# A state space scan laid out by channels, two heads side by side in the array's columns

## The chip, the cores and the metric

The kernel runs on one core of a Trainium2 chip. The metric is the device time of one execution in microseconds (us). The engines are TensorE (PE in the profile; its weight loads are PEld), VectorE (DVE), ScalarE (ACT), GpSimd (POOL) and SyncE (SP, which here only issues transfers). Each runs its own queue in order.

## The reference

One decoder layer for 256 tokens (T) of width 2048. The part that changes is the state space branch: 32 heads of 64 channels in 8 groups of 4 heads, each group with its own B and C of 128 states. All 256 tokens are one chunk, so the scan is one masked product:

```python
a_dt = dt * a                                  # a = -exp(a_log), per head
a_cum = cumsum(a_dt)                           # along the tokens
decay_in = exp(where(l >= s, a_cum[l] - a_cum[s], -inf))
cb = einsum('lgn,sgn->gls', c_in, b_in)
y = einsum('gls,gels,sgep->lgep', cb, decay_in, x * dt)
y = y + d_skip * x
g = y * silu(z)                                # 2048 channels in 8 groups of 256
o_ssd = g * rsqrt(mean(g * g, group) + 1e-6) * ssd_norm_w
...
merged = g_sb * (o_sb @ w_branch_sb) + g_ssd * (o_ssd @ w_branch_ssd) + g_mem * (o_mem @ w_branch_mem)
```

Before it come an RMSNorm and one wide input projection (for z, x, B, C, the other branches and the gates); beside it stand two attention branches, behind it an output projection, a residual and a last RMSNorm.

## The kernel before, in words

**Weights and gemms.** All weights stream from memory as fp32, 512 KB a chunk. A chunk is split into two fp32r parts: ScalarE copies `raw` to `wh`, VectorE subtracts and writes `wl` (`split`). Four `raw` buffers and three of each part are in use in turn. Two helpers multiply:

- `gemm` (rows: tokens on the output's partitions) holds 128 tokens of the activations still and streams 512 weight columns, three matmuls for each k tile and half of the tokens (L264 to L266). A chunk has two k tiles, 12 matmuls.
- `gemm_cols` (columns: channels on the output's partitions) holds 128 x 128 weights still and streams the tokens: two matmuls of 512 columns (both parts of the activations) and two of 256 (L227, L231) for each k tile. A chunk has four k tiles. The two accumulators are added by `fold`, one ScalarE copy and one VectorE addition for 256 channels.

**Order.** The order of all engines' work is the order in which the Python code issues it. After each chunk a gemm calls `pump()`: it runs what `defer` put off for so many chunks (the evacuations, the SiLUs), and then one step of one of two `lanes`. A lane is a queue of generators, and each `yield` ends a step, so small work is strewn between the chunks. Even chunks serve one lane, odd chunks the other. `finish()` runs what is left in the lanes without chunks between.

**The state space branch.** z is projected by `gemm` (rows, 4 calls) into `zD`, and x, B and C by `gemm_cols` (columns) with a causal convolution of four taps into `cT`; SiLU follows on both. `start_ssd` then puts 8 `ssd_group` generators and 8 `ssd_cols` into the lanes; they run between the chunks of the gates and branch products of the memory and stick-breaking branches. A group transposes x to rows (`xp`), loads the cumulated log decays of its four heads spread over all partitions (`dec`, from a small tensor `acT` in memory), makes the decays of the two diagonal 128 x 128 blocks (add, minimum, Exp), weighs them with the masked product of B and C (`cb`, `cbm`), and multiplies with x times dt (`xs`) into `y`, a matmul of 64 columns per head and block. The block below the diagonal needs no array of decays: x times dt is scaled by `edge[:, 0]`, multiplied once for all four heads (`off`), and scaled by `edge[:, 1]`. Then come the skip (`drow`), the gate, the sum of squares per token and 1 / rms by a power on GpSimd (`rsqrt_mean`). `ssd_cols` transposes the result back to columns (`dot`) and splits it into `oD`, the activations of `w_branch_ssd`.

Names with `wh`, `wl`, `acc` in the rows are the gemms; `hT`, `oM`, `oS`, `oD` and `mT` are their activations; `sig` are the gates, `merged` the sum of the branches.

Of the kernel before, what the change touches and what calls it, by code (L numbers as in the profile page):

```python
# [41 lines left out]
def trunk_kernel(  # L42
# [3 lines left out]
    d_skip, w_mem_kv, w_branch_sb, w_branch_ssd, w_branch_mem,  # L46
# [46 lines left out]
    wcols = const.tile([P, 192], F32, name="wcols")  # L93
    normw, ssdw, convb = wcols[:, 0:16], wcols[:, 16:32], wcols[:, 32:64]
    convw = wcols[:, 64:192].rearrange("p (j i) -> p j i", i=32)

# [27 lines left out]
    drow = const.tile([P, SSD_HEADS], F32, name="drow")  # L124

# [6 lines left out]
    edge = const.tile([P, 2, SSD_HEADS], F32, name="edge")  # L132
# [222 lines left out]
    def along(k):  # L355
# [14 lines left out]
        if k == 6:  # L370
            nc.sync.dma_start(wcols, w_cols)
            nc.sync.dma_start(drow, d_skip.partition_broadcast(P))
# [74 lines left out]
    def dt_steps():  # L447
# [222 lines left out]
    zD = [slot([P, D], F32, "zD") for _ in range(2)]  # L670

    def z_evac(c0):
        def evac(acc):
            for t in range(2):
                nc.scalar.activation(zD[t][:, c0:c0 + GW], acc[t], AF.Copy)
        return evac

    for g in range(4):
        gemm(hT, NKT, w_in, C_SSDZ + g * GW, z_evac(g * GW))
# [20 lines left out]
    waiting = [zD[i // 2][:, (i % 2) * 1024:(i % 2 + 1) * 1024] for i in range(4)]  # L700
# [11 lines left out]

    def ssd_group(g):
        heads = slice(4 * g, 4 * g + 4)
        cs = slice(g * T, (g + 1) * T)
        xp = bank([P, 2, T], "xp")
        for b in range(2):
            i = 2 * g + b
            for t in range(2):
                nc.tensor.transpose(xp[:, t, b * P:(b + 1) * P],  # L720
                                    cT[i // 8][:, i % 8, t * P:(t + 1) * P], ident)
        dec = []
        for h0 in (4 * g, 4 * g + 2):
            d = ta([P, 2, 2, P], "dec")
            nc.scalar.dma_start(d.rearrange("p h q t -> p h (q t)"),
                                acT[h0:h0 + 2].partition_broadcast(P))
            dec.append(d)
        yield
        xn = tb([P, 2, T], "xn")
        nc.scalar.activation(xn, xp, AF.Copy)  # L730
        xs = tb([P, 2, T], "xs")
        xe = tq([P, 3, P], "xe")
        by_head = lambda a: a.rearrange("p (h c) -> p h c", c=64)
        wide = lambda a: a[:, heads].unsqueeze(2).to_broadcast([P, 4, 64])
        xoff = xe[:, 0:2].rearrange("p a b -> p (a b)")
        for t in range(2):
            nc.gpsimd.tensor_tensor(by_head(xs[:, t]), by_head(xn[:, t]), wide(dts[:, t]),
                                    ALU.mult)
            nc.gpsimd.tensor_tensor(by_head(xn[:, t]), by_head(xn[:, t]), wide(drow), ALU.mult)
        nc.gpsimd.tensor_tensor(by_head(xoff), by_head(xs[:, 0]), wide(edge[:, 0]), ALU.mult)  # L740
        cb = bank([P, 4, P], "cb")
        bT, cTT = cT[2], cT[3]
        nc.tensor.matmul(cb[:, 0:2], bT[:, g, 0:P], cTT[:, g], start=True, stop=True)
        nc.tensor.matmul(cb[:, 2], bT[:, g, P:T], cTT[:, g, P:T], start=True, stop=True)
        yield

        for i, d in enumerate(dec):
            for e in range(2):
                for q in range(2):
                    h = 4 * g + 2 * i + e  # L750
                    nc.vector.tensor_scalar(d[:, e, q], d[:, e, q], nac[:, q, h:h + 1], 0.0,
                                            ALU.add, ALU.min)
        yield
        for d in dec:
            nc.scalar.activation(d, d, AF.Exp)
        yield
        nc.scalar.activation(xe[:, 2], cb[:, 1], AF.Copy)
        cbm = small2([P, 2, P], "cbm")
        nc.vector.tensor_tensor(cbm, cb[:, 0:3:2], past.unsqueeze(1).to_broadcast([P, 2, P]),
                                ALU.mult)  # L760
        for d in dec:
            nc.vector.tensor_tensor(d, d, cbm.unsqueeze(1).to_broadcast([P, 2, 2, P]),
                                    ALU.mult)
        yield
        y = bank([P, 2, T], "y")
        for e in range(4):
            xc = slice(e * 64, (e + 1) * 64)
            for q in range(2):
                nc.tensor.matmul(y[:, q, xc], dec[e // 2][:, e % 2, q], xs[:, q, xc], start=True, stop=True)  # L769
        off = bank([P, T], "off")  # L770
        nc.tensor.matmul(off, xe[:, 2], xoff, start=True, stop=True)  # L771
        yield
        nc.vector.tensor_tensor(by_head(xoff), by_head(off), wide(edge[:, 1]), ALU.mult)
        nc.vector.tensor_tensor(xn[:, 1], xn[:, 1], xoff, ALU.add)
        nc.vector.tensor_tensor(xn, y, xn, ALU.add)
        ss = small([P, 2], "gss")
        for t in range(2):
            nc.vector.tensor_tensor(xn[:, t], xn[:, t], zD[t][:, cs], ALU.mult)
        yield
        for t in range(2):  # L780
            nc.scalar.activation(xs[:, t], xn[:, t], AF.Square, accum_out=ss[:, t:t + 1])
        rs = small([P, 2], "grs")
        rsqrt_mean(rs, ss, T, 2)
        yield
        for t in range(2):
            nc.scalar.activation(zD[t][:, cs], xn[:, t], AF.Copy, scale=rs[:, t:t + 1])
        ssd_done.append(g)
        yield

    def ssd_cols(g):  # L790
# [4 lines left out]
        ot = bank([P, 2, T], "dot")  # L795
        for b in range(2):
            c = (2 * g + b) * P
            for t in range(2):
                nc.tensor.transpose(ot[:, b, t * P:(t + 1) * P], zD[t][:, c:c + P], ident)  # L799
        yield  # L800
        split(*[(*oD[0].at(2 * g + b), ot[:, b], ssdw[:, 2 * g + b:2 * g + b + 1])
                for b in range(2)])
# [22 lines left out]
    def gate_evac(c0, sig):  # L825
        nc.scalar.dma_start(sig[:, 0], b_gate[c0:c0 + GW].partition_broadcast(P))
        def evac(acc):
            for t in (1, 0):
                nc.vector.tensor_tensor(sig[:, t], acc[t], sig[:, 0], ALU.add)
            defer(lambda: nc.scalar.activation(sig, sig, AF.Sigmoid), 1)  # L830
# [18 lines left out]
    for br, (g0, src, nk, wb) in enumerate(branches):  # L849
        if br == 2:  # L850
            finish()
            mT.append(Cols(NKT, "mT"))
            src = oD[0]
        for g in range(4):
            sig = t4([P, 2, GW], "sig")
            gemm(hT, NKT, w_in, C_GATE + g0 + g * GW, gate_evac(g0 + g * GW, sig))
            gemm(src, nk, wb, g * GW, branch_evac(br, g, sig))
# [86 lines left out]
_INS = ['x', 'mem', 'x_cols', 'mem_cols', 'w_cols', 'w_in', 'b_gate', 'dt_bias', 'a_log', 'd_skip',  # L944
# [5 lines left out]
def lay_out(inputs):  # L950
# [10 lines left out]
    a['mem_cols'] = _np.concatenate([a['mem_norm_w'].reshape(-1, P).T, a['mem_cols']], axis=1)  # L961
    a['w_cols'] = _np.concatenate([a[n].reshape(-1, P).T for n in
# [19 lines left out]
```

## Time and profile before

| what | value |
|---|---|
| median of 3 runs | 1231.93 us (1231.27 to 1232.45) |
| profiled execution | 1232.29 us, span 1230.6 us |
| granted TensorE clock | 0.998 |
| busy: TensorE, its weight loads | 99%, 84% of the span |
| busy: VectorE, ScalarE, GpSimd | 62%, 50%, 7% |
| transfers | 240.58 MB, 196 GB/s |
| z projection (`zD`) | about 395 to 482 us |
| the groups and `ssd_cols` on TensorE | 685 to 948 us |

Busy time is a union over overlapping instructions. Matmuls are pipelined, and their recorded ends are modelled: two that follow each other overlap in the records, so the cost of one in a full queue is the distance from its start to the next start. An fp32 matmul is recorded as two passes, each with a weight load of its own. A row of the time order has the start, the duration, the engine, the line, the output and inputs, the tile sizes and the number of merged instructions; a row of waits has who waited, for whom, and the total, number and longest.

### The profile page before, as it was taken

Reading aid. Unit: us, or ns where it says so; the run is one execution under the profiler, and the core shown is the slowest. Engines: PE = TensorE matmul, PEld = TensorE weight load, DVE = VectorE, ACT = ScalarE, POOL = GpSimd, SP = SyncE. Lnnn points to the kernel's source line nnn. Section 1 sums busy time; section 2 is a strip of 40 time slices with the busy share of each in tenths; the row PEclk is TensorE's granted clock in tenths of the full one; section 3 lists DMA queues with packets and bytes.
Section 4 is the critical chain, followed back from the end, with each engine's and each line's share of the span. In section 5 each row is a group of like instructions: output and inputs, shape, how many; then the busy total and the mean of one; then the engine's idle time right before and its main releaser. Section 6 shows DMA issues by size and latency. Waiting matters only on the chain.

```text
span 1230.6 us, 16254 instructions
## 1 busy us (share of the span) xinstructions
PE 1220.5 (99%) x6228; PEld 1037.9 (84%) x6228; DVE 769.0 (62%) x999; ACT 617.2 (50%) x797; POOL 92.2 (7%) x104
## 2 busy tenths in 40 slices
PE   9999999999999999999999999999999999999997
PEld 7888888888888888888888888888888888888886
DVE  5686554565654555888878767576756554555554
ACT  6765544554444554545664655455555444444443
POOL 0000000000000000010000202123101110110101
PEclk9999999999999999999999999999999999999999
DMA  9966566655566665655666756666565666567673
GB/s 339 334 198 188 163 195 189 187 168 166 165 183 191 178 177 179 184 176 171 178 182 201 226 178 207 204 191 198 180 186 180 198 197 200 187 197 243 205 243 109
DMA packets 165789, 240.58 MB, mean 196 GB/s; under 512 B 10288, under 2 KB 93392, under 8 KB 165584
## 3 DMA queue, kind: packets, MB, share of 16 engines
q1 hardware_dynamic: 157152, 223.88, 58.9%
q10 hardware_dynamic: 8560, 15.67, 3.8%
q8 instruction: 48, 0.79, 0.3%
q14 instruction: 29, 0.24, 0.1%
HBM read 237.40 MB, written 2.13 MB: 195 GB/s over the span
## 4 chain that ended last, share of the span: by engine, by line
PE 95%; DMA 2%; issue 1%; ACT 1%; DVE 1%; SPq 0%; POOLq 0%; POOL 0%; ACTq 0%
PE acc L227 24%; PE acc L264 17%; PE acc L266 17%; PE acc L265 17%; PE acc L231 12%; PE y L769 1%; PE acc L400 1%; PE acc L401 1%; PE acc L399 1%; DMA raw<-in_w_out_dram 1%; DMA rows<-in_mem_dram 1%; DMA raw<-in_w_mem_kv_dram 0%; PE off L771 0%; PE dtp L459 0%; PE dot L799 0%
## 5 line engine op out<-in xcount | busy, mean ns | idle before, releaser
L148 DVE TENSOR_TENSOR wl<-raw,wh 128x1024 fp32r<-128x1024 f32 (+1 forms) x409 | 506.0, 1240 | 326.4 <-ACT wh L144 324.1
L144 ACT ACTIVATE wh<-raw 128x1024 fp32r<-128x1024 f32 (+1 forms) x409 | 431.5, 1056 | 423.7 <-PE acc L266 253.7
L227 PE MATMUL acc<-hT,wh 128*128 128x512 f32 x1152 | 363.2, 397 | 0.0
L231 PEld LDWEIGHTS acc<-hT,wl 128*128 128x128 f32 x1152 | 216.4, 188 | 51.2
L264 PE MATMUL acc<-wh,hT 128*128 128x512 f32 x576 | 227.8, 395 | 0.0
L231 PE MATMUL acc<-hT,wl 128*128 128x256 f32 x1152 | 226.5, 278 | 0.0
L266 PE MATMUL acc<-wh,hT 128*128 128x512 f32 x576 | 224.5, 390 | 0.0
L265 PE MATMUL acc<-wl,hT 128*128 128x512 f32 x576 | 224.4, 390 | 0.0
L227 PEld LDWEIGHTS acc<-hT,wh 128*128 128x128 f32 x1152 | 175.5, 189 | 0.1
L266 PEld LDWEIGHTS acc<-wh,hT 128*128 128x128 f32 x576 | 108.1, 188 | 22.9
L265 PEld LDWEIGHTS acc<-wl,hT 128*128 128x128 f32 x576 | 108.3, 188 | 21.8
L264 PEld LDWEIGHTS acc<-wh,hT 128*128 128x128 f32 x576 | 108.2, 188 | 21.7
L265 PE MATMUL acc<-wl,oD 128*128 128x512 f32 x128 | 49.8, 389 | 0.0
L266 PE MATMUL acc<-wh,oD 128*128 128x512 f32 x128 | 49.8, 389 | 0.0
L264 PE MATMUL acc<-wh,oD 128*128 128x512 f32 x128 | 49.8, 389 | 0.0
L695 DVE SCALAR_TENSOR_TENSOR cT<-cu,wcols,cT 128x255 f32<-128x255 f32 (+2 forms) x96 | 46.4, 483 | 3.4
L841 POOL TENSOR_TENSOR merged<-merged,sig 128x512 f32<-128x512 f32 x16 | 27.5, 1743 | 260.7 <-DVE sig L840 233.9
L631 POOL TENSOR_TENSOR lm<-lm,sp 128x384 f32<-128x384 f32 x8 | 11.5, 1432 | 394.5 <-DVE sp L630 392.4
L227 PE MATMUL acc<-memT,wh 128*128 128x512 f32 x128 | 40.6, 398 | 0.0
L264 PE MATMUL acc<-wh,mT 128*128 128x512 f32 x96 | 37.4, 390 | 0.0
L266 PE MATMUL acc<-wh,mT 128*128 128x512 f32 x96 | 37.4, 389 | 0.0
L265 PE MATMUL acc<-wl,mT 128*128 128x512 f32 x96 | 37.4, 389 | 0.0
(250 smaller groups left out, 1306.1 us busy)
## 6 DMA issues: line engine op xcount, KB each, us to landing
raw<-in_w_in_dram SPq DMA_DIRECT2D x288, 512.0 KB, 3.8
raw<-in_w_branch_ssd_dram SPq DMA_DIRECT2D x32, 512.0 KB, 4.0
raw<-in_w_out_dram SPq DMA_DIRECT2D x32, 512.0 KB, 4.9
raw<-in_w_mem_kv_dram SPq DMA_DIRECT2D x31, 512.0 KB, 6.3
raw<-in_w_branch_mem_dram SPq DMA_DIRECT2D x16, 512.0 KB, 4.8
raw<-in_w_branch_sb_dram SPq DMA_DIRECT2D x16, 512.0 KB, 4.3
dec<-acT ACTq DMA_DIRECT2D x16, 256.0 KB, 5.6
sig<-in_b_gate_dram ACTq DMA_DIRECT2D x12, 256.0 KB, 3.9
```

What stands on the lines that cost most here:

```text
L144: nc.scalar.activation(hi, src, AF.Copy, **({} if scale is None else {"scale": scale}))
L148: nc.vector.tensor_tensor(lo, src, h32, ALU.subtract)
L227: nc.tensor.matmul(halves[b], wh[:, kt - k0, b * P:(b + 1) * P], lhs.both(kt), start=first, stop=False, skip_group_check=True)
L231: nc.tensor.matmul(halves[b][:, 1], wl[:, kt - k0, b * P:(b + 1) * P], lhs.at(kt)[0], start=False, stop=last, skip_group_check=True)
L264: nc.tensor.matmul(a, lh[:, tt], wh[:, j], start=first, stop=False)
L265: nc.tensor.matmul(a, lh[:, tt], wl[:, j], start=False, stop=False)
L266: nc.tensor.matmul(a, ll[:, tt], wh[:, j], start=False, stop=last)
L399: nc.tensor.matmul(a, lh[:, tt], wh[:, g], start=first, stop=False)
L400: nc.tensor.matmul(a, lh[:, tt], wl[:, g], start=False, stop=False)
L401: nc.tensor.matmul(a, ll[:, tt], wh[:, g], start=False, stop=last)
L695: nc.vector.scalar_tensor_tensor(a[:, s:T], u[:, 0:T - s], convw[:, 3 - s, i:i + 1], a[:, s:T], ALU.mult, ALU.add)
L841: nc.gpsimd.tensor_tensor(merged[t][:, cs], merged[t][:, cs], sig[:, t], ALU.add)
```

## The change

The state space branch now stays in columns. z is projected by `gemm_cols` into `zT`. In a group, x is still transposed for use as the stationary operand, but now x times dt (64 columns of a head) is held still and the weighed decays are streamed, so `y` comes out with channels on partitions: two heads go to partitions 0 to 63 and 64 to 127 of the output, that is to the two halves of the array's columns. The decays of the block below the diagonal are made like the others (`nacx` in place of `edge`), three blocks a head; the four heads' blocks lie in three tiles `dec`, one of them from another pool. The loads of `dec` are issued by SP instead of ScalarE, five of 128 or 64 KB instead of two of 256 KB. The skip is one VectorE operation per 128 channels with a column `dcol` that comes with `wcols`. The sum of squares over the 256 channels of a group is now one across partitions: squares, an addition, a split, and two matmuls with ones (`rb`) into `tot`. 1 / rms is exp(-0.5 ln(ms)) on ScalarE and one step of Newton's on VectorE, both on 128 x 256 elements. `ssd_cols` has no transposes any more. `exp_ln` loads the table that has both Exp and Ln if a Sigmoid has been there since. `finish()` and the allocation of `mT` stand behind the first gate product of the third branch instead of ahead of it.

```diff
-    zD = [slot([P, D], F32, "zD") for _ in range(2)]
...
-    for g in range(4):
-        gemm(hT, NKT, w_in, C_SSDZ + g * GW, z_evac(g * GW))
+    zT = [slot([P, 8, T], F32, "zT") for _ in range(2)]
+    for g in range(8):
+        gemm_cols(hT, NKT, w_in, C_SSDZ + 2 * g * P, to_cols(zT[g // 4], 2 * (g % 4)))
...
-        nc.vector.tensor_tensor(edge[:, 0], nac[:, 0], ps[:, 2], ALU.subtract)
-        nc.vector.tensor_scalar(edge[:, 1], nac[:, 1], -1.0, None, ALU.mult)
-        nc.scalar.activation(edge, edge, AF.Exp)
+        nc.vector.tensor_tensor(nacx, nac[:, 0], ps[:, 2], ALU.subtract)
...
+    def exp_ln():
+        if not tables[0]:
+            nc.scalar.preload_act_table_set("natural_log_exp_and_others")
+            tables[0] = True
...
     def ssd_group(g):
+        dec = [ta([P, 4, P], "dec"), ta([P, 4, P], "dec"), tb([P, 4, P], "dec")]
+        block = lambda e, j: dec[e][:, j] if e < 3 else dec[j][:, 3]
+        for e in range(3):
+            nc.sync.dma_start(dec[e][:, 0:2].rearrange("p q t -> p (q t)"),
+                              acT[heads[e]:heads[e] + 1].partition_broadcast(P))
+        for j in range(2):
+            nc.sync.dma_start(dec[j][:, 3:4], acT[heads[3]:heads[3] + 1,
+                                                  j * P:(j + 1) * P].partition_broadcast(P))
...
+        nc.vector.tensor_tensor(by_head(xs), by_head(xp), dts[:, :, heads[0]:heads[0] + 4]
+                                .unsqueeze(3).to_broadcast([P, 2, 4, 64]), ALU.mult)
...
+        def log_decays(e):
+            for j, i, a in ((2, 1, nac[:, 1]), (1, 1, nacx), (0, 0, nac[:, 0])):
+                nc.vector.tensor_scalar(block(e, j), block(e, i), a[:, heads[e]:heads[e] + 1],
+                                        0.0, ALU.add, ALU.min)
+        def weigh(i):
+            nc.vector.tensor_tensor(dec[i][:, 0:3], dec[i][:, 0:3], cbm, ALU.mult)
+            nc.vector.tensor_tensor(dec[i][:, 3], dec[i][:, 3], cbm[:, i], ALU.mult)
...
         y = bank([P, 2, T], "y")
-        for e in range(4):
-            xc = slice(e * 64, (e + 1) * 64)
-            for q in range(2):
-                nc.tensor.matmul(y[:, q, xc], dec[e // 2][:, e % 2, q], xs[:, q, xc], start=True, stop=True)
-        off = bank([P, T], "off")
-        nc.tensor.matmul(off, xe[:, 2], xoff, start=True, stop=True)
+        for b in range(2):
+            pair = [(e, y[64 * (e % 2):64 * (e % 2) + 64, b]) for e in (2 * b, 2 * b + 1)]
+            xe = lambda e, t: xs[:, t, 64 * e:64 * e + 64]
+            for e, o in pair:
+                if e < 3:
+                    nc.tensor.matmul(o, xe(e, 0), dec[e][:, 0:2], start=True, stop=False,
+                                     skip_group_check=True)
+                else:
+                    for j in range(2):
+                        nc.tensor.matmul(o[:, j * P:(j + 1) * P], xe(e, 0), block(e, j),
+                                         start=(j == 0), stop=False, skip_group_check=True)
+            for e, o in pair:
+                nc.tensor.matmul(o[:, P:T], xe(e, 1), block(e, 2), start=False, stop=True,
+                                 skip_group_check=True)
...
+            nc.vector.scalar_tensor_tensor(xT[b], xT[b], dcol[:, i:i + 1], y[:, b], ALU.mult,
+                                           ALU.add)
...
+        nc.vector.tensor_tensor(zg, zg, xg, ALU.mult)
+        nc.scalar.activation(xs, zg, AF.Square)
+        yield
+        nc.vector.tensor_tensor(xs[:, 0], xs[:, 0], xs[:, 1], ALU.add)
+        sq = tmp.tile([P, 2, T], F32R, tag="tq", name=nm("sq"), bufs=2)
+        split((sq[:, 0], sq[:, 1], xs[:, 0], None))
+        yield
+        tot = bank([P, T], "tot")
+        for i in range(2):
+            nc.tensor.matmul(tot, rb, sq[:, i], start=(i == 0), stop=(i == 1))
+        yield
+        ms, rs = xs[:, 0], xs[:, 1]
+        nc.vector.tensor_scalar(ms, tot, 1.0 / T, EPS, ALU.mult, ALU.add)
+        exp_ln()
+        nc.scalar.activation(rs, ms, AF.Ln)
+        nc.scalar.activation(rs, rs, AF.Exp, scale=-0.5)
+        yield
+        nc.vector.tensor_tensor(ms, ms, rs, ALU.mult)
+        nc.vector.tensor_tensor(ms, ms, rs, ALU.mult)
+        nc.vector.tensor_scalar(ms, ms, -0.5, 1.5, ALU.mult, ALU.add)
+        nc.vector.tensor_tensor(rs, rs, ms, ALU.mult)
+        nc.vector.tensor_tensor(zg, zg, xs[:, 1:2].to_broadcast([P, 2, T]), ALU.mult)
...
     def ssd_cols(g):
-            for t in range(2):
-                nc.tensor.transpose(ot[:, b, t * P:(t + 1) * P], zD[t][:, c:c + P], ident)
+        split(*[(*oD[0].at(i), zT[i // 8][:, i % 8], ssdw[:, i:i + 1])
+                for i in (2 * g, 2 * g + 1)])
```

How this moves instructions is shown at three places. First TensorE at the diagonal step of the third group, before:

```order
L266 MATMUL acc_6637<-wh_6708,oM_2162 128x512
L769 MATMUL y_6725<-xs_6525,dec_6472 128x64 x4
L769 MATMUL y_6725<-xs_6525,dec_6474 128x64 x4
L771 MATMUL off_6734<-xe_6526 128x256
L264 MATMUL acc_6738<-wh_6741,hT_122 128x512
```

and after, where the size is that of the output (64 channels by 256 or 128 tokens):

```order
L265 MATMUL acc_6893<-wh_6918,hT_121 128x512
L779 MATMUL y_6934<-dec_6658,xs_6731 64x256
L779 MATMUL y_6934<-dec_6659,xs_6731 64x256
L786 MATMUL y_6934<-dec_6658,xs_6731 64x128
L786 MATMUL y_6934<-dec_6659,xs_6731 64x128
L779 MATMUL y_6934<-dec_6660,xs_6731 64x256
L783 MATMUL y_6934<-dec_6658,xs_6731 64x128
L783 MATMUL y_6934<-dec_6659,xs_6731 64x128
L786 MATMUL y_6934<-dec_6660,xs_6731 64x128 x2
L263 MATMUL acc_6893<-wh_6946,hT_122 128x512
```

Nine matmuls stand where nine stood; eight of 64 columns and one of 256 became three of 256 and six of 128, and heads take turns in the queue. Second TensorE in the z projection, before:

```order
L264 MATMUL acc_3577<-wh_3580,hT_122 128x512
L265 MATMUL acc_3577<-wl_3581,hT_122 128x512
L266 MATMUL acc_3577<-wh_3580,hT_122 128x512
L264 MATMUL acc_3577<-wh_3580,hT_122 128x512
L265 MATMUL acc_3577<-wl_3581,hT_122 128x512
L266 MATMUL acc_3577<-wh_3580,hT_122 128x512
```

and after, behind a step of a stick-breaking head (`slg`):

```order
L612 MATMUL slg_3475<-qS_2159,kS_2160 128x2x128
L613 MATMUL slg_3475<-qS_2159,kS_2160 128x128
L226 MATMUL acc_3403<-hT_124,wh_3480 128x512 x2
L230 MATMUL acc_3403<-hT_124,wl_3481 128x256 x2
L226 MATMUL acc_3403<-hT_124,wh_3480 128x512 x2
L230 MATMUL acc_3403<-hT_124,wl_3481 128x256 x2
```

The same product is made from pairs of 512 and 256 columns instead of triples of 512. Third VectorE where the second step of a group falls, before (log decays of two groups between the weights' `wl`):

```order
L148 TENSOR_TENSOR wl_6568<-raw_6565,wh_6567 128x1024
L751 TENSOR_SCALAR dec_6472<-dec_6472,nac 128x128 x4
L751 TENSOR_SCALAR dec_6474<-dec_6474,nac 128x128 x4
L148 TENSOR_TENSOR wl_6594<-raw_6591,wh_6593 128x1024
L751 TENSOR_SCALAR dec_6501<-dec_6501,nac 128x128 x4
L751 TENSOR_SCALAR dec_6503<-dec_6503,nac 128x128 x4
L148 TENSOR_TENSOR wl_6620<-raw_6617,wh_6619 128x1024
```

and after, where an evacuation of a branch product (`merged`) comes in between:

```order
L147 TENSOR_TENSOR wl_7235<-raw_7232,wh_7234 128x1024
L741 TENSOR_TENSOR xs_7250<-xp_7182,dts 128x512
L745 TENSOR_TENSOR cbm_7252<-cb_7187,past 128x2x128
L751 TENSOR_SCALAR dec_7174<-dec_7174,nac 128x128
L751 TENSOR_SCALAR dec_7174<-dec_7174,nacx 128x128
L147 TENSOR_TENSOR wl_7261<-raw_7258,wh_7260 128x1024
L862 TENSOR_TENSOR merged_5974<-acc_7083,sig_6891 128x512
L862 TENSOR_TENSOR merged_5975<-acc_7083,sig_6891 128x512
L741 TENSOR_TENSOR xs_7278<-xp_7224,dts 128x512
L745 TENSOR_TENSOR cbm_7280<-cb_7229,past 128x2x128
```

What stood on GpSimd (the scaling of x) and in later steps has moved into the steps of two groups that follow each other here; nine more log decays of each group follow in the two chunks behind.

More of the change, by code (lines that the diff above doesn't have):

```diff
@@ L698, in conv_evac @@
         return evac
-    waiting = [zD[i // 2][:, (i % 2) * 1024:(i % 2 + 1) * 1024] for i in range(4)]
+    waiting = [zT[i // 2][:, 4 * (i % 2):4 * (i % 2) + 4] for i in range(4)]
     for i, g in enumerate((4, 5, 6, 7, 0, 1, 2, 3)):
@@ L728, in ssd_group @@
[L728 to L739, printed above, removed]
@@ L758, in ssd_group @@
[L758 to L763, printed above, removed]
+        exp_ln()
+        nc.scalar.activation(dec[1], dec[1], AF.Exp)
+        nc.scalar.activation(dec[2], dec[2], AF.Exp)
+        weigh(0)
+        yield
+        weigh(1)
```

96 lines of the change are left out of this document (38 added, 58 removed).

## The prediction

> **What bounds the kernel now.** I read the page first, then TensorE's waits, then the order of time on TensorE around the steps that change, then VectorE and ScalarE there.
>
> ```profile
> PE 1220.5 (99%) x6228; PEld 1037.9 (84%) x6228; DVE 769.0 (62%) x999; ACT 617.2 (50%) x797; POOL 92.2 (7%) x104
> PEclk9999999999999999999999999999999999999999
> PE 95%; DMA 2%; issue 1%; ACT 1%; DVE 1%; SPq 0%; POOLq 0%; POOL 0%; ACTq 0%
> PE warm L109 <- POOL ones L98: 1.0, 1, 1.0
> PE acc L400 <- DVE wl L148: 0.6, 2, 0.4
> PE acc L937 <- DVE yo L868: 0.2, 1, 0.2
> ```
>
> The first row gives TensorE (PE) 99% of the span, at the full granted clock all along; the chain that ended last is PE for 95%. The last three rows are all that TensorE waited for: 1.8 us, and nothing in the state space stage (664 to 950 us). So work taken off TensorE's queue shortens the span by itself, work added lengthens it, and the other engines count only where they would make TensorE wait for the first time. I therefore price every edit by its slots in TensorE's order, from start to start: the durations of single matmuls overlap.
>
> **The rows for the prices.** First the diagonal step of one group of heads, then the product of B and C, both in time order on TensorE; then the first and last of eight transposing steps.
>
> ```profile
> 714.98 0.39 PE L266 MATMUL acc<-wh,hT 128*128 128x512 f32 x1
> 715.21 1.89 PE L769 MATMUL y<-xs,dec 128*128 128x64 f32 x16
> 716.94 0.65 PE L771 MATMUL off<-xe 128*128 128x256 f32 x2
> 717.24 0.59 PE L264 MATMUL acc<-wh,hT 128*128 128x512 f32 x1
> 717.66 0.40 PE L265 MATMUL acc<-wl,hT 128*128 128x512 f32 x1
> ...
> 692.09 0.59 PE L743 MATMUL cb<-cT,cT 128*128 128x256 f32 x2
> 692.52 0.38 PE L744 MATMUL cb<-cT,cT 128*128 128x128 f32 x2
> 692.66 0.47 PE L264 MATMUL acc<-wh,oM 128*128 128x512 f32 x1
> 692.97 0.39 PE L265 MATMUL acc<-wl,oM 128*128 128x512 f32 x1
> ...
> 909.20 0.44 PE dot L799 x4
> 948.03 0.44 PE dot L799 x4
> ```
>
> Every fp32 matmul stands as two passes (x2, x16 for 8). Now the pace of the two gemm helpers (29 rows from 395.44 to 401.81; four k tiles from 330.30 to 333.09), of 256-column fp32r matmuls, and of the one place that already uses a stationary operand of 64 columns.
>
> ```profile
> 395.44 0.39 PE L265 MATMUL acc<-wl,hT 128*128 128x512 f32 x1
> 401.81 0.39 PE L266 MATMUL acc<-wh,hT 128*128 128x512 f32 x1
> ...
> 330.30 0.62 PE L227 MATMUL acc<-hT,wh 128*128 128x512 f32 x2
> 333.09 0.63 PE L227 MATMUL acc<-hT,wh 128*128 128x512 f32 x2
> ...
> 333.78 0.28 PE L578 MATMUL mpo<-mph,vh 128*128 128x256 f32 x1
> 335.10 0.28 PE L580 MATMUL mpo<-mph,vl 128*128 128x256 f32 x1
> ...
> 109.01 1.07 PE L459 MATMUL dtp<-hT,wd 128*64 128x256 f32 x8
> 109.92 0.63 PE L227 MATMUL acc<-hT,wh 128*128 128x512 f32 x2
> ```
>
> **The change on TensorE, step by step.**
>
> Removed, `y` and `off`: from 714.98 to 717.66 is 2.68 us, less two ordinary steps of (401.81 - 395.44) / 28 = 0.2275 us: 2.22 us a group, 17.8 us for 8. Removed, the transposes of `ssd_cols`: 8 x 0.44 = 3.5 us. `xp` and `cb` stay as they are.
>
> Added, `tot`: two fp32r matmuls of 256 columns at (335.10 - 333.78) / 11 = 0.12 us, 0.24 us a group, 1.9 us in all.
>
> The z projection goes from `gemm` to `gemm_cols`. For 512 columns `gemm` issues 96 matmuls x 0.2275 = 21.84 us; `gemm_cols` twice 16 k tiles x (333.09 - 330.30) / 4 = 0.6975 us, 22.32 us. Four times the difference: +1.9 us.
>
> So far -17.8 - 3.5 + 1.9 + 1.9 = -17.5 us, and the new `y` has to be paid from it. It has no row: heads lie in halves of the array, 64 columns of stationary operand each. Its passes have a price: by L743 a 256-column fp32 matmul takes 692.52 - 692.09 = 0.43 us, 0.215 a pass (call it u), and by L744 (0.14, and 0.08 that the next step is late) a 128-column one 0.22 us. A group has three of the former and six of the latter, 12u. Upper end, the halves take turns: 2.6 us a group, 20.8 us. Lower end, the halves are always both busy: 6u, 1.3 us, 10.4 us. Between them lies what an ordered queue gives if the halves can run at once: nothing starts before the instruction ahead of it has started, and a half's own passes follow each other. Head 0 holds its half from 0 to 2u, and head 1 can only start with head 0's second pass: u to 3u. The two 128-column matmuls run from 2u to 3u and 3u to 4u. Head 2 starts at 3.5u and ends at 5.5u; head 3's four short passes take 4.5u to 6.5u; the last two matmuls end at 7u and 7.5u. That is 1.61 us a group, 12.9 us. I take it: queue order is what every row above shows, while side by side is shown by none; both ends stay for the range. The new `y` breaks even at 17.5 / 8 = 2.19 us a group.
>
> Net: +3.3 (turns), -4.6 (staggered), -7.1 (both always busy).
>
> The matrix changes its shape twice a group (128 columns to 64 and back). L459 is the nearest row: 8 matmuls in 109.92 - 109.01 = 0.91 us, 0.114 each against 0.12 for full width, so entering and leaving cost nothing visible: 0. The upper end is an emptied pipeline, 0.39 - 0.2275 = 0.16 us a change, 16 times, 2.6 us. The Trainium skill, TensorEngine Tiling (Array Packing), Key Properties, speaks against the change here: it says that changing the tiling mode drains the array. By the row the sum stays at -4.6, by the rule it would be about -2.0; the L459 row does not agree with it for fp32r, and no row tests fp32.
>
> **The change beside TensorE.** VectorE and ScalarE prepare the weights (`wh`, `wl`), and TensorE would wait if that came late.
>
> ```profile
> 664.00:906.00 242.00, 242.00 (x1156) 202.88 (x1155) 166.74 (x240) 129.55 (x177) 45.64 (x60) 1.00 0.62 195
> 748.52 3.11 DVE L751 TENSOR_SCALAR dec<-dec,nac 128x128 f32<-128x128 f32 x8
> 752.68 1.65 DVE L751 TENSOR_SCALAR dec<-dec,nac 128x128 f32<-128x128 f32 x8
> 754.25 1.21 DVE L148 TENSOR_TENSOR wl<-raw,wh 128x1024 fp32r<-128x1024 f32 x1
> ...
> 773.47 0.42 DVE L773 TENSOR_TENSOR xe<-off,edge 128x256 f32<-128x256 f32 x1 [2.57 <-PE off L771]
> 773.93 0.43 DVE L774 TENSOR_TENSOR xn<-xn,xe 128x256 f32<-128x256 f32 x1
> 774.39 0.69 DVE L775 TENSOR_TENSOR xn<-y,xn 128x512 f32<-128x512 f32 x1
> 738.50 1.28 DVE L838 TENSOR_TENSOR merged<-acc,sig 128x512 f32<-128x512 f32 x2
> ACT wh L144 <- PE acc L266: 253.7, 156, 3.9
> L755 ACT ACT_TABLE_LOAD x4 | 5.1, 1283 | 0.1
> L725 ACTq DMA_DIRECT2D dec<-acT x16: 326/424/757, 677.7 to 848.4; - x16
> SPq L205 <- DVE wl L148: 877.4, 348, 5.7
> ```
>
> In the first row VectorE (third busy time) is at work 166.74 of 242 us. A group now adds the scaling of x (0.7), a twelfth instead of an eighth log decay (4 x 0.2), the sums of squares, Newton's four (0.46 a dependent 256-column step) and a 512-column product, and loses `xe`, `xn` and their kin: about 11.2 us against 6.4, +38 us in all, 205 of 242. Average room stays; a burst decides. The worst is where two groups end and two begin with an evacuation between (the third piece of order): two times 2.4 us (Newton and the gating), two times 1.85 (x, `cbm`, three decays), 1.28 (L838), two times 1.8 (nine decays at 0.2), six `wl` at 1.24, together 20.9 us for six `wl`. ScalarE starts `wh` when TensorE frees a buffer three chunks back (the 253.7 us wait), and `wh` + `wl` take 2.3 us, so before the burst `wl` is ready at 2.3 us on a clock on which TensorE wants the sixth one 8 chunks of 2.73, two inserted `xp` and `cb` (1.1 each) and one step later, at 24.3. 2.3 + 20.9 = 23.2: 1.1 us to spare. With the decays at L751's slower 0.39 (eight in 3.11, beside GpSimd, which the change relieves) it is 2.3 us short. Three such bursts: 0 to 7 us. I take 0.5 us in all, near the faster row, since GpSimd has only `merged` left.
>
> ScalarE: 4 us a group as before; each of 8 sigmoids may now force a reload of the exponential table, some 7 more x 1.28 = 9 us against 112 us idle there: 0. If it met a burst, its 1.28 us would add to the shortage. The Ln waits for VectorE's `ms` with the next `wh` queued behind it, and the Square waits for the gating alike: under 2.5 us, inside the two chunks of lead (5.5 us).
>
> The `dec` loads leave ScalarE's queue (two issues of 0.42) for SP's, five a group, between weight loads. SP waits 877.4 / 348 = 2.5 us before a load, so 5 x 0.42 = 2.1 us falls into waiting: 0; without that cover the next `raw` would come 2.1 us later, out of the same lead. Bytes are equal. The z fold adds 8 VectorE operations of 0.69 in a stage with VectorE half idle. `drow`, `edge` and the GpSimd steps lay on nobody's path: 0. Moving `finish()` behind the first gate product gives the lanes 8 more chunks: no cost, and no gain, since TensorE waits nowhere there.
>
> Sum: -4.6 + 0.5 = -4.1. The profiled execution took 1232.29 us (span 1230.6 and 1.7 around it), 0.36 above the median 1231.93; so 1228.2 by it and 1227.8 by the median: I say 1228.
>
> **Rivals.** (a) The halves take turns, so nothing runs side by side: 20.8 us for `y`, and with 0.5 us 1232.3 + 3.8 = 1236.1, slower. For it: no row shows two matmuls at once. It decides from 2.43 us a group on (11.3u), where the loss passes 0.2%. (b) Both halves always busy: 10.4 us, 1225.7. Against it: the in-order argument. The Trainium skill's TensorEngine Tiling, Key Properties, lets different tiles load and multiply in parallel, which bears out the overlap of (b) as of my forecast; no run here shows it yet. (c) Overlap as forecast, with 2.6 us lost to drained shape changes (the rule above) or as much in VectorE's bursts: 1230.8, within 0.2%.
>
> **How the numbers follow.** Staggered 0.43, (a) 0.28, (b) 0.12, (c) 0.17. About 0.2%, 2.5 us, is what a measurement of this kernel can tell. Faster: 0.38 of the staggered, all of (b): 0.50. Slower: 0.24 of (a) and 0.04 of (c), if its losses pile up: 0.28. Same: the rest, 0.22. The range reaches from below (b) to above (a) with some 2 us of bursts: 1224.5 to 1238; for the faster cases alone 1225 to 1229.5.
>
> **What would show it.** The slots of `y` from the matmul before to the second behind: 1.6 us more than ordinary is my case, 2.6 is (a), 1.3 is (b). `dot` gone, `tot` at 0.24, the z stage 1.9 us longer. TensorE's waits between 664 and 950 us naming `wl` would be (c). I am wrong if the passes of 64-wide fp32 matmuls are themselves slower than 0.215 us, or if VectorE leaves TensorE waiting for several us.

## The result, and the profile after

The changed kernel takes 1242.95 us, median of 4 runs (1242.26 to 1243.05), against 1232.19 (1231.27 to 1234.18) for the kernel before in the same session: ratio 1.0084 [1.0066, 1.0101]. It is 10.8 us slower, where 4 us faster was forecast.

The page of the changed kernel, its busy times and its chain; then its waits of TensorE:

```profile
PE 1220.9 (98%) x6340; PEld 1031.9 (83%) x6340; DVE 806.8 (65%) x1126; ACT 624.3 (50%) x786; POOL 52.8 (4%) x48
PE 87%; DVE 5%; ACT 3%; DMA 3%; issue 2%; SPq 0%; ACTq 0%; POOLq 0%; POOL 0%; DVEq 0%
```

```profile
PE acc L264 <- DVE wl L147: 8.7, 14, 1.2
PE acc L398 <- DVE wl L147: 0.9, 3, 0.4
```

The chain that ended last now leaves TensorE for 13% of its length (5% before), and a wait for `wl` that the kernel before did not have stands at the head: 14 times, 8.7 us. That figure is too small, since a wait shows only once the modelled end of the matmul ahead has passed. At the wait shown further below, the starts on both sides (734.21 and 735.70) are 1.49 us apart where two ordinary steps take 0.455: 1.03 us were lost, 0.76 are recorded. With 0.27 more each, the 14 waits are some 12.5 us.

So I compare the stage. From its first gate product to the first product on `oD` (663.87 to 978.28 before, 665.39 to 987.74 after) TensorE takes 322.35 us where it took 314.41: +7.9. By the instructions alone, with `y` as now measured, it should take 6.2 less (-17.8 - 3.5 + 1.9 + 13.2). Some 14 us of this stage are lost, about what the waits for `wl` come to. The two spans differ by 10.7 us. Of the rest, 1.5 lie ahead of the stage (1.9 more in the z projection, 0.4 less ahead of it) and 1.3 behind it (253.6 against 252.3). The experiments with four `raw` buffers leave that last part alone and have 251.8 to 253.5 there, so I put it down to no step of the change.

The new `y` itself, in time order on TensorE:

```profile
717.01 0.39 PE L265 MATMUL acc<-wh,hT 128*128 128x512 f32 x1
717.33 0.65 PE L779 MATMUL y<-dec,xs 128*64 128x256 f32 x4
717.81 0.39 PE L786 MATMUL y<-dec,xs 128*64 128x128 f32 x4
718.03 0.38 PE L779 MATMUL y<-dec,xs 128*64 128x256 f32 x1
718.04 0.38 PE L783 MATMUL y<-dec,xs 128*64 128x128 f32 x2
718.25 0.38 PE L779 MATMUL y<-dec,xs 128*64 128x256 f32 x1
718.25 0.38 PE L783 MATMUL y<-dec,xs 128*64 128x128 f32 x2
718.46 0.39 PE L786 MATMUL y<-dec,xs 128*64 128x128 f32 x4
718.78 0.50 PE L263 MATMUL acc<-wh,hT 128*128 128x512 f32 x1
719.12 0.39 PE L264 MATMUL acc<-wl,hT 128*128 128x512 f32 x1
```

From 717.01 to 719.12 is 2.11 us, less two ordinary steps 1.655 us a group, 13.2 us in all; all eight groups take the same to 0.002 us. The first row of `y` holds four passes in two steps: both heads of the pair at once. Head 3's first short passes (L783) start at 718.04, while head 2's second pass (L779), ahead of them in the code, starts at 718.25.

Where the waiting comes from shows behind `y`. A stretch of the changed kernel's time order, on ScalarE, VectorE and TensorE; a row ends with the idle time ahead of it and who ended it:

```profile
720.59 0.63 ACT L795 ACTIVATE xs<-zT 128x512 f32<-128x512 f32 x1 [4.81 <-DVE zT L794]
721.13 1.04 ACT L143 ACTIVATE wh<-raw 128x1024 fp32r<-128x1024 f32 x1
725.03 0.63 ACT L795 ACTIVATE xs<-zT 128x512 f32<-128x512 f32 x1 [2.86 <-DVE zT L794]
725.57 1.04 ACT L143 ACTIVATE wh<-raw 128x1024 fp32r<-128x1024 f32 x1
...
715.81 1.23 DVE L147 TENSOR_TENSOR wl<-raw,wh 128x1024 fp32r<-128x1024 f32 x1 [1.05 <-ACT wh L143]
718.90 0.87 DVE L791 SCALAR_TENSOR_TENSOR cT<-cT,wcols,y 128x256 f32<-128x256 f32 x2 [1.86 <-PE y L786]
719.80 0.69 DVE L794 TENSOR_TENSOR zT<-zT,cT 128x512 f32<-128x512 f32 x1
722.20 1.23 DVE L147 TENSOR_TENSOR wl<-raw,wh 128x1024 fp32r<-128x1024 f32 x1 [1.71 <-ACT wh L143]
723.34 0.87 DVE L791 SCALAR_TENSOR_TENSOR cT<-cT,wcols,y 128x256 f32<-128x256 f32 x2
724.25 0.69 DVE L794 TENSOR_TENSOR zT<-zT,cT 128x512 f32<-128x512 f32 x1
726.64 1.22 DVE L147 TENSOR_TENSOR wl<-raw,wh 128x1024 fp32r<-128x1024 f32 x1 [1.71 <-ACT wh L143]
...
734.08 1.23 DVE L147 TENSOR_TENSOR wl<-raw,wh 128x1024 fp32r<-128x1024 f32 x1 [0.52 <-ACT wh L143]
...
734.21 0.39 PE L263 MATMUL acc<-wh,oM 128*128 128x512 f32 x1
735.36 0.50 PE L264 MATMUL acc<-wl,oM 128*128 128x512 f32 x1 [0.76 <-DVE wl L147]
735.70 0.40 PE L265 MATMUL acc<-wh,oM 128*128 128x512 f32 x1
```

ScalarE stands 4.81 us before the Square, because VectorE has not gated `y` yet (VectorE itself waited for `y`, 1.86 us). The next `wh`, with which the Square has nothing to do, comes only behind it, and VectorE then idles 1.71 us for that `wh`. The two engines have become one chain: from the `wl` of 722.20 to that of 726.64 it is `wl` 1.14 us, skip and gate 1.69, Square 0.54, `wh` 1.07, 4.44 us, where TensorE wants a `wl` every 2.73. Neither engine is full; each waits for the other in turn, and at 735.36 the stock is gone and TensorE waits. Five steps of a group stand so (waits of ScalarE in the changed kernel: total, times, longest; the Square, the split, the copy of `cb`, the first Exp, the Ln):

```profile
ACT wh L143 <- PE acc L265: 178.1, 114, 3.1
...
ACT xs L795 <- DVE zT L794: 28.3, 8, 4.8
ACT sq L143 <- DVE xs L797: 18.1, 8, 3.7
ACT cbm L744 <- PE cb L737: 17.9, 8, 2.7
ACT dec L763 <- DVE dec L751: 16.7, 7, 4.1
ACT xs L810 <- DVE xs L808: 13.9, 8, 2.9
```

Together 94.9 us, all in the stage. The first row is the healthy wait, for a free buffer, which means that ScalarE is ahead. Its fall over the whole execution (253.7 us before, 178.1 now) overstates the loss, since 31.7 us of it belonged to the z projection, which now waits by a row of `gemm_cols`. In the stage alone it is 96.5 us before, 47.2 in the changed kernel and 85.9 with all five steps put off (below). The stock of ready weights went into the other five. Such waits alone are not the harm: the kernel before had two of them, for `xp` and `dot`, 28.2 us together, and TensorE waited for nothing in the stage.

### The profile page after: what moved, and what is told of

Same layout as the page of the kernel before. It is cut to its first block, busy times and chain, and to the rows that moved or that the text cites. A ratio compares the mean times of both kernels' runs of the same rounds, so it can differ in the third digit from the quotient of the medians.

```text
span 1241.3 us, 16565 instructions
## 1 busy us (share of the span) xinstructions
PE 1220.9 (98%) x6340; PEld 1031.9 (83%) x6340; DVE 806.8 (65%) x1126; ACT 624.3 (50%) x786; POOL 52.8 (4%) x48
## 4 chain that ended last, share of the span: by engine, by line
PE 87%; DVE 5%; ACT 3%; DMA 3%; issue 2%; SPq 0%; ACTq 0%; POOLq 0%; POOL 0%; DVEq 0%
PE acc L226 29%; PE acc L230 14%; PE acc L264 12%; PE acc L263 12%; PE acc L265 12%; DVE wl L147 2%; ACT wh L143 1%; PE acc L398 1%; DMA raw<-in_w_out_dram 1%; PE acc L399 1%; PE acc L397 1%; DMA rows<-in_mem_dram 1%; DMA dec<-acT 1%; PE y L779 1%; DVE dec L751 0%
## 5 line engine op out<-in xcount | busy, mean ns | idle before, releaser
L143 ACT ACTIVATE wh<-raw 128x1024 fp32r<-128x1024 f32 (+1 forms) x409 | 430.0, 1054 | 345.2 <-PE acc L265 178.1
L226 PE MATMUL acc<-hT,wh 128*128 128x512 f32 x1408 | 444.0, 397 | 0.0
L230 PEld LDWEIGHTS acc<-hT,wl 128*128 128x128 f32 x1408 | 264.5, 188 | 62.5
L230 PE MATMUL acc<-hT,wl 128*128 128x256 f32 x1408 | 276.8, 278 | 0.0
L226 PEld LDWEIGHTS acc<-hT,wh 128*128 128x128 f32 x1408 | 214.5, 189 | 0.1
L264 PE MATMUL acc<-wl,hT 128*128 128x512 f32 x448 | 176.0, 393 | 6.7 <-DVE wl L147 6.7
L263 PE MATMUL acc<-wh,hT 128*128 128x512 f32 x448 | 176.0, 393 | 0.4 <-ACT wh L143 0.4
L265 PE MATMUL acc<-wh,hT 128*128 128x512 f32 x448 | 174.6, 390 | 0.0
L264 PEld LDWEIGHTS acc<-wl,hT 128*128 128x128 f32 x448 | 84.1, 188 | 28.6 <-DVE wl L147 12.2
L263 PEld LDWEIGHTS acc<-wh,hT 128*128 128x128 f32 x448 | 84.1, 188 | 18.8 <-issue 1.0
L265 PEld LDWEIGHTS acc<-wh,hT 128*128 128x128 f32 x448 | 84.1, 188 | 17.4
```

Of the source, the lines that this page charges most:

```text
L143: nc.scalar.activation(hi, src, AF.Copy, **({} if scale is None else {"scale": scale}))
L226: nc.tensor.matmul(halves[b], wh[:, kt - k0, b * P:(b + 1) * P], lhs.both(kt), start=first, stop=False, skip_group_check=True)
L230: nc.tensor.matmul(halves[b][:, 1], wl[:, kt - k0, b * P:(b + 1) * P], lhs.at(kt)[0], start=False, stop=last, skip_group_check=True)
L263: nc.tensor.matmul(a, lh[:, tt], wh[:, j], start=first, stop=False)
L264: nc.tensor.matmul(a, lh[:, tt], wl[:, j], start=False, stop=False)
L265: nc.tensor.matmul(a, ll[:, tt], wh[:, j], start=False, stop=last)
```

## The experiments

The theories: (A) ScalarE waits in its queue for VectorE or TensorE with the next `wh` behind it. (B) VectorE's greater load, in bursts, is the cost by itself. (C) SyncE's five loads of `dec` a group hold up `raw`. Each kernel is an edit of the changed one. The kernel before had medians of 1233.06, 1232.73, 1232.76 and 1233.25 us in the four sessions of the experiments; times of different sessions are set side by side below without correction for that.

**All five ScalarE steps one chunk later.** Nothing is left out and the counts stay; `defer(..., 1)` puts the step behind the next chunk's `wh`. The split takes its VectorE subtraction along; the other four move ScalarE's work alone.

```diff
-        nc.scalar.activation(cbm[:, 1], cb[:, 1], AF.Copy)
+        defer(lambda: nc.scalar.activation(cbm[:, 1], cb[:, 1], AF.Copy), 1)
...
+        defer(lambda: (exp_ln(), nc.scalar.activation(dec[0], dec[0], AF.Exp)), 1)
+        defer(lambda: nc.scalar.activation(xs, zg, AF.Square), 1)
+        defer(lambda: split((sq[:, 0], sq[:, 1], xs[:, 0], None)), 1)
+        defer(lambda: (exp_ln(), nc.scalar.activation(rs, ms, AF.Ln),
+                       nc.scalar.activation(rs, rs, AF.Exp, scale=-0.5)), 1)
```

> The changed kernel with five ScalarE steps (the copy of cb, the first Exp, the Square, the split of the squares, Ln and Exp) put off by one chunk each, behind one more weight copy; no work is added or removed. Theory A (ScalarE waits in its queue for a result that VectorE or TensorE makes in the same step, with the next weight copy behind it, and the lead of the weights is lost): most of the 14 us of waiting goes, 1228 to 1232 us. Theory B (VectorE has too much work in its bursts): the work is the same, 1240 to 1243 us. Theory C (the ten loads of decays on SP's queue hold up the weight loads): 1241 to 1243 us.

1229.37 us (1228.68 to 1231.47, 10 runs), ratio 0.9973 [0.9963, 0.9982]: 13.6 us less than the changed kernel, and faster than the kernel before. The stage takes 308.6 us, 5.8 less than before, near the 6.2 of its instructions. VectorE does the same work there (242.1 us busy in the stage, 241.6 in the changed kernel), and the loads of `dec` are still SyncE's: that speaks against B and C, which had expected 1240 to 1243. Waits of TensorE and of ScalarE there:

```profile
PE acc L264 <- DVE wl L147: 0.3, 1, 0.3
...
ACT xs L794 <- DVE zT L793: 16.0, 8, 2.1
ACT cbm L744 <- DVE cbm L745: 8.2, 6, 3.0
```

The same place in this kernel, on ScalarE and VectorE: `wh` is made (719.59) while VectorE waits for `y`, and the next `wl` follows the gating without a gap, ahead of the Square.

```profile
719.59 1.06 ACT L143 ACTIVATE wh<-raw 128x1024 fp32r<-128x1024 f32 x1 [1.66 <-PE acc L265]
722.75 0.63 ACT L794 ACTIVATE xs<-zT 128x512 f32<-128x512 f32 x1 [2.10 <-DVE zT L793]
...
717.97 1.23 DVE L147 TENSOR_TENSOR wl<-raw,wh 128x1024 fp32r<-128x1024 f32 x1 [1.49 <-ACT wh L143]
721.96 0.69 DVE L793 TENSOR_TENSOR zT<-zT,cT 128x512 f32<-128x512 f32 x1
722.57 1.22 DVE L147 TENSOR_TENSOR wl<-raw,wh 128x1024 fp32r<-128x1024 f32 x1
...
732.68 1.22 DVE L147 TENSOR_TENSOR wl<-raw,wh 128x1024 fp32r<-128x1024 f32 x1
```

From the `wl` ahead of the gating to the fourth behind it, it is 14.71 us (717.97 to 732.68); the changed kernel needs 18.27 (715.81 to 734.08).

**Parts of that edit.** The Square, the split and the Ln with its Exp alone:

> Only the three ScalarE steps at a group's end (Square, split of the squares, Ln and Exp) are put off by one chunk; the copy of cb and the first Exp stay. These three hold 60 of the 95 us that ScalarE waited in its queue. Theory A: about 60% of the way, 1234 to 1237 us. Theories B and C: 1240 to 1243 us.

1231.64 us (1230.96 to 1234.61, 10 runs), 0.9992 [0.9982, 1.0002], more of the way than A's 1234 to 1237. The other two alone:

> The changed kernel with only the two early steps one chunk later (the copy of cb, the first Exp of the decays). Their waits were 17.9 + 16.7 of the 95 us that ScalarE waited with a wh behind. Theory A by shares of those waits: 36% of the 13.6 us, 1238. If the two ends only add up (the three late steps alone gained 11.3 of 13.6): 2.3 us, 1240.6. If instead the lead is one stock that either half of the edit mostly saves, more than 8 us: under 1235.

1240.77 us (1238.75 to 1241.3, 4 runs), 1.0064 [1.0047, 1.0081], as the sum of the two ends gave (1240.6), and not as the shares did (1238). And the Square alone:

> The changed kernel with the Square alone one chunk later, the others as they are. It had 28.3 of the 60.3 us that ScalarE waited at the three late steps, which gained 11.3 us together. By share: 5.3 us, 1237.6. If each wait matters only by what is queued behind VectorE there, and the Square stands behind the longest run of VectorE work: 7 to 9 us, 1234 to 1236. If the waits only pass on to the next step (the split, which then waits longer): under 2 us, 1241 to 1243.

1237.31 us (1237.02 to 1237.87, 5 runs), 1.0035 [1.0022, 1.0048], as the share gave (1237.6). Here one ScalarE instruction a group moved and nothing of VectorE's, and 5.6 us went. The two halves add up, 11.3 + 2.2 of 13.6 us. The rows of ScalarE's waits tell why the early half gives less than its share: the copy of `cb` now waits 15.2 us for `cbm` in place of 17.9 for `cb`, so that only the Exp's wait fell much (16.7 to 6.1). Sums of the five waits against the stage and the time:

| kernel | the five waits, us | stage, us | time, us |
|---|---|---|---|
| changed | 94.9 | 322.35 | 1242.95 |
| copy and first Exp later | 81.6 | 319.75 | 1240.77 |
| Square later | 78.6 | 316.97 | 1237.31 |
| Square, split, Ln later | 51.8 | 311.85 | 1231.64 |
| all five later | 29.8 | 308.62 | 1229.37 |

Time falls with the waits, by 0.16 to 0.35 us for each us of them, and the time goes in the stage: the lead pays for most of a wait, and TensorE for what is beyond it.

**Newton's step left out**, four VectorE operations of 256 columns a group (the output loses the step's accuracy):

```diff
-        nc.vector.tensor_tensor(ms, ms, rs, ALU.mult)
-        nc.vector.tensor_tensor(ms, ms, rs, ALU.mult)
-        nc.vector.tensor_scalar(ms, ms, -0.5, 1.5, ALU.mult, ALU.add)
-        nc.vector.tensor_tensor(rs, rs, ms, ALU.mult)
```

> The changed kernel without Newton's step: 1 / rms is the plain exponential of the logarithm, and four dependent VectorE operations of 0.33 to 0.46 us a group (13 us in all) are gone. Theory B: the bursts at the ends of the groups lose 3.3 us of VectorE work in two chunks, and half or more of the waiting goes, 1233 to 1238 us. Theory A: 1240 to 1243 us, since no wait of ScalarE is touched. Theory C: 1242 to 1243 us.

1237.42 us (1236.73 to 1238.09, 4 runs), 1.0041 [1.0027, 1.0056], 5.5 us less than the changed kernel. That is what B wants, and A in the form in which it was written (1240 to 1243) missed it: the five waits still come to 90.8 us, so VectorE's work counts here beside them, in the chain of the two engines. But the same edit on top of the five deferred steps:

> The kernel with all five ScalarE steps one chunk later, and Newton's four VectorE steps left out as well (1 / rms is the logarithm's and exponential's own). Theory A (the time went because ScalarE waited in its queue for VectorE or TensorE with the next wh behind it): once these waits are apart, VectorE's work is covered, and since TensorE waits only 0.3 us for wl there, taking 1.85 us of VectorE's work off each group gains at most 0.5 us: 1228.9 to 1229.4. Theory B (VectorE's load in bursts is the cost by itself): the 5.5 us that the same edit gained alone come again, 1224 to 1226.

1228.31 us (1227.3 to 1228.8, 4 runs), 0.996 [0.9946, 0.9975], 1.1 us less than with Newton's step in, and the two intervals overlap. That is a little below A's 1228.9 and well above B's 1226. VectorE's work costs time while the five waits use up the lead; taken by itself it is nearly covered. B falls as a cause of its own and stays as a link of A.

**1 / rms left out as a whole**, logarithm, exponential and Newton's step; the sums over channels stay:

> The changed kernel with 1 / rms left out as a whole: neither logarithm nor exponential nor Newton's four steps, the output is scaled by the mean square instead; everything else stays, the sums over channels too. This splits the change's cost between its two parts. Newton alone gave 5.5 us. Theory A adds the wait of the Ln in ScalarE's queue, at the 0.21 to 0.35 us of time for a us of such waits that the other runs showed, 13.9 x 0.21 to 0.35 = 2.9 to 4.9 us, and some of ScalarE's own 0.8 us a group: 1232 to 1234.5. Theory B (VectorE's load alone): the same VectorE steps are gone as with Newton left out, 1237.4.

1234.45 us (1233.74 to 1235.95, 10 runs), 1.0013 [1.0003, 1.0022]. That is 8.5 us less than the changed kernel and 3.0 less than without Newton's step alone, at the end of the range that A gave. So more than half of the loss goes when 1 / rms goes; the Square, the split, the Exp and the copy still wait (TensorE still waits 2.6 us for `wl`). The parts overlap and must not be added: the Square alone gave 5.6 us. Nor is it the Ln's wait alone: with the logarithm, 6 of the stage's 15 table loads on ScalarE (1.28 us each) went too, and a group has one step less.

**The loads of `dec` on ScalarE's queue**, as the kernel before had them (theory C):

```diff
-            nc.sync.dma_start(dec[e][:, 0:2].rearrange("p q t -> p (q t)"),
+            nc.scalar.dma_start(dec[e][:, 0:2].rearrange("p q t -> p (q t)"),
```

> The changed kernel with the five loads of decays of a group issued by ScalarE again instead of SP. Theory C: the weights arrive in time again, 1230 to 1236 us. Theories A and B: no gain, and ScalarE has 2 us more to issue per group: 1242 to 1246 us.

1251.32 us (1249.48 to 1254.54, 4 runs), 1.0157 [1.0139, 1.0175], 8.4 us more, above what any of the theories gave. C falls: SyncE's route helped. Waits and time order of ScalarE in this kernel:

```profile
ACT wh L143 <- DMA dec<-acT: 22.8, 4, 6.6
...
751.44 4.81 ACTq L727 DMA_DIRECT2D dec<-acT  x2
756.29 1.06 ACT L143 ACTIVATE wh<-raw 128x1024 fp32r<-128x1024 f32 x1 [5.45 <-DMA dec<-acT]
```

Two issues stood 4.81 us in ScalarE's queue, with `wh` behind them: the same fault by another cause. Whether they waited for a free tile or for the queue of transfers the rows do not tell.

**The halves of `y` in another order**: heads 0 and 2 (the lower half of the columns) first, then 1 and 3, on top of the five deferred steps.

```diff
+        for e in (0, 2, 1, 3):
+            o = y[64 * (e % 2):64 * (e % 2) + 64, e // 2]
```

> All five ScalarE steps one chunk later, and the matmuls of y in another order: heads 0 and 2 (the lower half of the columns) first, then heads 1 and 3. Same instructions, same count. If the halves take from one queue in which a matmul starts only when the ones ahead of it have started, the lower half's 6u run nearly alone and the upper half's 6u after them: about 2.5 us a group instead of 1.3, +9 to +10 us, 1238 to 1239.5. If each half takes its own matmuls as they come, however far back they stand: 1229.4.

1235.5 us (1234.16 to 1236.68, 10 runs), 1.0021 [1.0011, 1.003], 6.1 us more than in the paired order: between the two expectations. `y` in that kernel:

```profile
719.02 0.39 PE L265 MATMUL acc<-wh,hT 128*128 128x512 f32 x1
719.34 0.65 PE L777 MATMUL y<-dec,xs 128*64 128x256 f32 x2
719.82 0.38 PE L783 MATMUL y<-dec,xs 128*64 128x128 f32 x2
720.04 0.65 PE L777 MATMUL y<-dec,xs 128*64 128x256 f32 x4
...
721.50 0.50 PE L263 MATMUL acc<-wh,hT 128*128 128x512 f32 x1
721.83 0.39 PE L264 MATMUL acc<-wl,hT 128*128 128x512 f32 x1
```

Head 0 runs alone (719.34, 719.82: two passes a row where the paired order had four), then heads 2 and 1 together at 720.04. 721.83 - 719.02 less 0.455 is 2.36 us against 1.655: 0.70 more, 5.6 us in 8 groups. Head 1's first pass, ninth in the code, started beside the fifth and not beside the first: a half does take its matmuls past others that wait for the other half, but not from that far back. All eight groups take 2.36 us, so it is hardly a wait for data, which would differ from group to group.

**Two that decided nothing.** The power on GpSimd in place of logarithm, exponential and Newton's step:

> The changed kernel with 1 / rms by one power on GpSimd (128x256) in place of logarithm, exponential and Newton's four steps; the other waits stay as they are. Theory A: Newton's part as measured (5.5 us), and the Ln's wait (13.9 of 95 us, some 2 us of the loss) go as well, and no wh stands behind GpSimd: 1235 to 1236. Theory B (only VectorE's load counts): the same VectorE steps are gone as with Newton left out, so 1237.4. If GpSimd's work slows VectorE's beside it, more: 1238 to 1240.

1530.16 us (1529.9 to 1530.61, 4 runs). The groups and waits of this kernel say why:

```profile
L809 POOL TENSOR_TENSOR xs<-xs,mhalf 128x256 f32<-128x256 f32 x8 | 331.6, 41457 | 239.2 <-DMA dec<-acT 151.4 <-DVE xs L808 87.8
DVE zT L811 <- POOL xs L809: 307.6, 8, 41.0
```

One power over 128 x 256 elements takes 41.5 us, and VectorE, not ScalarE, waited 307.6 us for it; A and B are not told apart by it.

And a fourth buffer for `wh`, paid for with one of four for `raw`; the control has three for `raw` alone:

> The changed kernel with three buffers instead of four for the raw weights, a control for the next one (the buffer's room is needed there). The loads still run two chunks ahead, so little is expected from either theory: 1243 to 1245, 1 to 2 us more where SyncE's ten loads of decays meet a shorter stock.

> Three raw buffers, and four for wh instead of three, wl stays at three: ScalarE may run one chunk (2.73 us) further ahead, VectorE not. Theory A in its wide form (ScalarE's waits eat its lead of three chunks, and any more lead absorbs them): most waits are under 4.8 us, so more than half of the 13.6 us comes back against the control, 1234 to 1237. Theory A in its narrow form (ScalarE and VectorE are one chain in the stretches between waits, and VectorE's lead, bound by wl's three buffers, is what is lost): 2 to 5 us, 1239 to 1241. Theory B (VectorE's load): nothing, as the control.

The control took 1251.73 us (1249.47 to 1252.07, 4 runs), where 1243 to 1245 was expected, and the fourth `wh` 1249.63 (1248.33 to 1251.23, 4 runs), a difference that the spread of the runs covers. The stage took 322.3 us in both (668.4 to 990.7; 669.1 to 991.4), as in the changed kernel. The control lost its 8.8 us outside it: in its profile the stage begins 3.0 us later, and what follows it takes 259.0 us in place of 253.6. There ScalarE waits 30.0 us for `raw` of the output projection, which it did not in the changed kernel. With the fourth `wh`, ScalarE's main wait is for loads:

```profile
ACT wh L143 <- DMA raw<-in_w_in_dram: 123.9, 86, 4.2
```

So it could not run further ahead; whether more lead would absorb the waits is open. Four buffers of each kind were not tried.

## Why the prediction was wrong

**The step that failed** is the one beside TensorE: "under 2.5 us, inside the two chunks of lead (5.5 us)" for the Ln and the Square, taken as 0, with 0.5 us for VectorE's bursts. Measured: 13.6 us, which went when these steps were put off by a chunk. Three things were wrong in it. I priced two of five steps, and left out the copy of `cb`, the first Exp and the split. I took waits of under 2.5 us, and the longest were 4.8, 4.1, 3.7, 2.9 and 2.7, since work of VectorE's (or `cb` on TensorE) stands ahead of each of them. And I held each wait against the full lead as if it stood alone: two groups run in turn, so a wait meets a lead that the one before has already used. My worst case of VectorE counted VectorE's work in a row and left ScalarE free to run ahead; a `wl` that waits for a `wh` that waits for VectorE was not in it. (By its own rule it was also too mild: its slower variant counts 18 of the 24 decays at 0.39 us; with all of them it is 3.5 us short and not 2.3, and three such bursts cost 10 us and not 7.) Rival (c) named VectorE's bursts, but at 2.6 us; the upper end of 7 us was still half of what came.

**`y`: forecast 12.9 us, measured 13.2, by luck: two errors cancel.** The argument for staggering, that nothing starts before the instruction ahead of it, is wrong between the halves: they overlap fully, as rival (b) had it (six passes of 0.215, 1.3 us a group; 717.33 to 718.68 is 1.35). The Trainium skill's TensorEngine Tiling (Array Packing), Key Properties, lets different tiles load and multiply in parallel; the trace agrees, four passes in two steps at 717.33. The other error is the change of shape, taken as 0 from L459: 717.01 to 717.33 is 0.09 us over an ordinary step, and leaving costs 0.10 (the last pair, at 718.46, should give way at 718.68 by two passes of 0.11 in each half, and the next starts at 718.78) and 0.11 more (718.78 to 719.12). That is 0.30 us a group, 2.4 us in all, close to the upper end of 2.6. The rule in the same section of the Trainium skill, that a change of mode drains the array, fits these rows. L459 was the wrong row to set against it: its matmuls use one half of the columns alone, and they are fp32r. Which of the two makes the difference, no run tells.

**The rest of TensorE's sum held.** With ScalarE's waits apart, the stage takes 5.8 us less than before, where the instructions give 6.2. The z projection takes 94.29 us on TensorE (382.58 to 476.87) where it took 92.36 (383.00 to 475.36; the table ahead has its evacuations rather): +1.93, as forecast, and the same in every kernel of the experiments. Their stages begin 1.4 to 5.2 us later than in the kernel before, and what differs lies ahead of the z projection: 0.6 us earlier to 2.3 later with four `raw` buffers, though up to there the instructions are the same, and that stays unexplained. Stage and z projection together are 3.9 us shorter with the five steps put off, where the forecast had 4.1. So 1228.0 was about what the change is worth (1229.37) once ScalarE's queue is freed.

**`dec` on SyncE at 0** is borne out in so far as the other route cost 8.4 us more; no run shows its own price. The reloaded tables (15 loads in the stage, 9 before) and the moved `finish()` have no run of their own; in the kernel with five deferred steps both stand and leave no visible loss.

## What to carry to other kernels

When an engine on the path's supply line runs in order, price each small step by what it may wait for and by what stands behind it in that queue, not by its own duration; a busy share of 50% says nothing about this. Issue such a step one chunk behind its inputs, so that the steady work goes first: here that turned a loss of 10.8 us into a gain of 3.7. And when a share of the wait for free buffers (96.5 to 47.2 us in the stage) moves to waits for another engine, read it as lead that is lost, even where TensorE's own recorded wait is still small. Take such a wait by stage: over the whole execution other changes are mixed in.

## What the hardware showed that I had not expected

Matmuls of the two column halves run side by side and past each other's order (718.04 before 718.25); but the ninth pass of a group started beside the fifth (720.04), not beside the first, so it pays to write heads in pairs (1.655 us a group against 2.36). Entering and leaving the 64-column shape costs 0.30 us a group in fp32. A power on GpSimd over 128 x 256 elements takes 41.5 us.
